# Eight column orders for the moving operand of the matmuls of fourteen weight matrices

## The chip, the cores and the metric

The kernel runs on one core of one Trainium2 chip. The metric is the device time of one execution in microseconds (us). The core has a matrix engine (TensorE, PE in the profile; its weight loads are listed as PEld), a vector engine (DVE), a scalar engine (ACT), GpSimd (POOL) and SyncE (SP), which issues most of the transfers. A matmul first loads a stationary operand into the array and then streams the columns of its moving operand past it; the sums land in a PSUM bank.

## The reference

Two transformer blocks of width 2048 run one after the other on 256 tokens, in fp32. Cut to the products with the fourteen matrices whose layout changes (names of the kernel behind the arrow):

```python
h = rmsnorm(x, g_mix)                        # first block
gate_sb, gate_ca = h @ w_in[...]             # -> w_gsb, w_gca
merged = (sigmoid(gate_sb) * (y_sb @ w_sb_out)      # -> w_sbo
          + sigmoid(gate_ca) * (y_ca @ w_ca_out))   # -> w_cao
x = x + merged @ w_mix_out                   # -> w_mix
x = x + (silu(g_ff) * u_ff) @ w_ffn_out      # -> w_fout
x = x + sigmoid(h @ w_ple_gate) * (p @ w_ple_in)    # -> w_pg
gates = hn @ w_in_2[...]                     # second block -> w_ga, w_gb, w_gc
z = gelu(y) @ w_glu                          # -> w_gluv, w_glug
h = h + merged @ w_out                       # -> w_out
h = h + conv_gated_mlp(...) @ ffn_w_down     # -> w_down
```

All fourteen products have 2048 output columns. Their depths are 2048, except 1024 for `w_sbo`, `w_cao`, `w_gluv` and `w_glug`, 5632 for `w_fout` and 5504 for `w_down`.

## The kernel before

The whole computation is one stream of jobs (`stream`, line 448). A job is one output tile of a product: it reads half tiles of weights, 128 partitions by 1024 fp32, and accumulates into `acc`, two PSUM banks of 512 columns, which exists twice so that the next job can start while the last one is read out.

Each half tile goes through three steps. `load` (L459) is a transfer of 512 KB that SP issues, into one of four `raw` buffers. `high` (L466) rounds it on ACT into `wh`, of type fp32r, a number that one matmul pass can multiply. `low` (L476) subtracts on DVE what was rounded away and rounds that into `wl`. The activations are kept as such a pair too: `hilo` (L318 and L319, or a scaled form at L310 and L313) makes it. A product is then the sum of three passes: high times high, high times low, and low times high. `high` runs four half tiles ahead of the matmuls (five `wh` buffers) and `low` three ahead (four `wl` buffers).

There are two main kinds of job. In a WS job (L526, L530) the weights are the stationary operand and the activations move. In an AS job the activations are stationary and the weights move: `mm_as` (L539) takes, for each of the two 128-row blocks `k` of a half tile and each of the two halves `m` of the 256 tokens, a plain slice of 512 neighbouring columns of `wh` or `wl` and issues three matmuls (L560 to L562). For the very first half tile (L550 to L553) the passes that need `wl` come last. The last job of all calls `mm_as` once per `m` (L509), so that half of the output can be finished early. All matmuls with the fourteen matrices are AS jobs, with four column tiles `n` of 512 columns each. `as_job` (L565) builds them; seven smaller matrices use it too and are not touched by the change.

`_as` (L53) lays an AS matrix out on the host: column tile by column tile, and in it half tile by half tile, 128 partitions by two rows of 512 columns. That is done before the measured time.

The order of the instructions is written out by hand. Beside the job stream, generators (the normalisations, attention heads, gated linear attention, a state-space scan, evacuations of `acc`) advance by one step after each half tile (`tick`); each engine runs its instructions in the order in which they were issued.

Of the kernel before, what the change touches and what calls it, by code (L numbers as in the profile page):

```python
# [35 lines left out]
def _ws(a, b):  # L36

    K, F = a.shape

    def blk(w):  # L40
        return w.reshape(K // 512, 4, 128, F // 128, 128).transpose(3, 0, 2, 1, 4)

    return np.concatenate([blk(a), blk(b)], axis=-1).reshape(-1, 128, 1024)


def _pairs(w):

    K, F = w.shape
    v = w.reshape(K, F // 256, 2, 128)
    return _ws(v[:, :, 0].reshape(K, F // 2), v[:, :, 1].reshape(K, F // 2))  # L50


def _as(w):  # L53
# [19 lines left out]
def layout(x, p, w_in, w_sb_out, w_ca_out, w_mix_out, rel_bias, g_mix, g_ffn, g_ple, g_final, w_ffn_in,  # L73
# [5 lines left out]
    a = {}  # L79
# [5 lines left out]
    i, j = np.arange(128)[:, None], np.arange(128)[None, :]  # L85
# [24 lines left out]
    w = w_in[0]  # L110
# [8 lines left out]

    w = w_in_2[0]  # L120
    a["w_u"] = _pairs(w[:, 0:1024])
    a["w_qkg"] = _ws(w[:, 1024:1536], w[:, 1536:2048])
    a["w_vg"], a["w_r"] = _as(w[:, 2048:3072]), _pairs(w[:, 3072:4096])

    alr = np.zeros((16, 128, 32), np.float32)
# [28 lines left out]
    a["s5b"] = b.reshape(128, 4, 2048).transpose(1, 0, 2)  # L154
    a["s5c"] = c.reshape(128, 2048)
    a["s5bt"] = bt.reshape(128, 2048)
    return {k: np.ascontiguousarray(v) for k, v in a.items()}


# [26 lines left out]
class Build:  # L186
# [261 lines left out]
    def stream(self, jobs):  # L448
        nc = self.nc
        halves = [(j, i, ks) for j in jobs for i, ks in j.halves]  # L450
        N = len(halves)
        raws, spl = {}, {}
        width = lambda j, ks: {"AS": 512 * len(ks), "WS": 1024, "W4": 512}[j.kind]

        def load(i):
            j, idx, ks = halves[i]
            n = width(j, ks)
            r = self.rawp.tile([128, 1024], F32, tag="raw", name=self.name("raw"))
            nc.sync.dma_start(out=r[:, :n], in_=self.d[j.w][idx][:, :n])  # L459
            raws[i] = r  # L460

        def high(i):
            j, idx, ks = halves[i]
            n = width(j, ks)
            wh = self.whp.tile([128, 1024], F32R, tag="wh", name=self.name("wh"))
            nc.scalar.copy(wh[:, :n] if j.kind != "W4" else wh[:, :n].bitcast(F32), raws[i][:, :n])  # L466
            spl[i] = wh

        def low(i):
            j, idx, ks = halves[i]  # L470
            n = width(j, ks)
            r, wh = raws.pop(i), spl[i]
            wl = None
            if j.kind != "W4":
                wl = self.wlp.tile([128, 1024], F32R, tag="wl", name=self.name("wl"))
                nc.vector.tensor_sub(wl[:, :n], r[:, :n], wh[:, :n].bitcast(F32))  # L476
            spl[i] = (wh, wl)
            if i + RAWB < N:
                load(i + RAWB)

        ahead = self.at_start(load)
        for i in range(CA):
            next(ahead)
            high(i)
            if i < SA:
                low(i)
        self.add(ahead)
        last, prev, acc = None, None, None
        for i, (j, idx, ks) in enumerate(halves):
            if i + CA < N:  # L490
                high(i + CA)
            if i + SA < N:
                low(i + SA)
            if j is not last:
                if j.before is not None:
                    j.before()
                while prev is not None and not prev.free:
                    self.tick(must=True)
                prev, last = last, j
                acc = self.accp.tile([128, 2, 512], F32, tag="acc", name=self.name("acc"))  # L500
            for k in ks:
                while k not in j.acts.ready:
                    self.tick(must=True)
            first, end = j.halves[0][1][0], j.halves[-1][1][-1]
            if j.by_m is not None:

                for m in range(2):
                    for q, (_, _, kq) in enumerate(halves[i:]):
                        self.mm_as(j.acts, kq, *spl[i + q], acc, (m,), first, end)  # L509
                    j.by_m(m, acc)  # L510
                break
            wh, wl = spl.pop(i)
            if j.kind == "AS":
                self.mm_as(j.acts, ks, wh, wl, acc, (0, 1), first, end, low_last=i == 0)
            elif j.kind == "W4":

                for k in range(16):
                    p = slice(32 * (k % 4), 32 * (k % 4) + 32)
                    nc.tensor.matmul(acc[p, 0, :], lhsT=wh[:, 32 * k:32 * k + 32].bitcast(F32),
                                     rhs=j.acts.at(k).bitcast(F32), start=k < 4, stop=k >= 12)  # L520
            else:
                for kk, k in enumerate(ks):
                    x = j.acts.at(k)
                    for f in range(2):
                        s = slice((kk * 2 + f) * 128, (kk * 2 + f) * 128 + 128)
                        hi = lambda: nc.tensor.matmul(  # L526
                            acc[:, f, :], lhsT=wh[:, s], rhs=x, start=k == first, stop=k == end)
                        if k == first:
                            hi()
                        nc.tensor.matmul(acc[:, f, 256:512], lhsT=wl[:, s], rhs=x[:, 0:256], start=False, stop=False)  # L530
                        if k != first:
                            hi()
            if i + 1 == N or halves[i + 1][0] is not j:
                self.add(j.evac(acc, lambda j=j: setattr(j, "free", True)), front=True)
            self.tick()
        while self.gens:
            self.tick(must=True)

    def mm_as(self, acts, ks, wh, wl, acc, ms, first, end, low_last=False):  # L539

        nc = self.nc
        if low_last:
            for low in (False, True):
                for kk, k in enumerate(ks):
                    s = slice(kk * 512, kk * 512 + 512)
                    for m in ms:
                        x = acts.at(k)
                        xh, xl = x[:, m * 128:m * 128 + 128], x[:, 256 + m * 128:384 + m * 128]
                        if low:
                            nc.tensor.matmul(acc[:, m, :], lhsT=xh, rhs=wl[:, s], start=False, stop=False)  # L550
                        else:
                            nc.tensor.matmul(acc[:, m, :], lhsT=xl, rhs=wh[:, s], start=k == first, stop=False)
                            nc.tensor.matmul(acc[:, m, :], lhsT=xh, rhs=wh[:, s], start=False, stop=False)  # L553
            return
        for kk, k in enumerate(ks):
            x = acts.at(k)
            s = slice(kk * 512, kk * 512 + 512)
            for m in ms:
                xh, xl = x[:, m * 128:m * 128 + 128], x[:, 256 + m * 128:384 + m * 128]
                nc.tensor.matmul(acc[:, m, :], lhsT=xl, rhs=wh[:, s], start=k == first, stop=False)  # L560
                nc.tensor.matmul(acc[:, m, :], lhsT=xh, rhs=wl[:, s], start=False, stop=False)  # L561
                nc.tensor.matmul(acc[:, m, :], lhsT=xh, rhs=wh[:, s], start=False, stop=k == end)  # L562


    def as_job(self, w, n, acts, evac, k0=0, nk=None, before=None, kt=None):  # L565

        kt = kt or acts.n
        nk = nk or acts.n
        per = (kt + 1) // 2
        halves = [(n * per + (k0 + k) // 2, list(range(k, min(k + 2, nk)))) for k in range(0, nk, 2)]  # L570
        return Job("AS", w, halves, acts, lambda acc, free: evac(n, acc, free), before)

    def ws_job(self, w, j, acts, evac, before=None):

# [1193 lines left out]
```

## Time and profile before

| | us |
|---|---|
| median of 2 runs | 3183.36 (3183.13 to 3183.58) |
| profiled execution, its own time | 3182.36 |
| its span | 3180.2 |
| PE busy | 3161.4 |
| DVE busy | 1994.4 |
| ACT busy | 1553.3 |

The span runs from the first to the last instruction. A line of the groups view names the source line, the engine, the operation, its output and inputs by tile name, the shape and the count; behind the bar stand the busy time in us, the mean duration of one in ns, and how long the engine had been idle just before, with what ended that wait. A line `min/median/max` gives durations in ns, and then the first and the last start in us from the span's beginning. A windows line gives, for one stretch, the busy time and the number of instructions of each engine, the granted clock of TensorE, and the share and the rate of the DMA engines. The matmuls overlap, so that their busy times add up to more than the time in which they run; a line of the page counts overlapping time once.

### The profile page before, as it was taken

To read this page: it belongs to the slowest core of one execution; us is meant where nothing else is said; L and a number is where in the kernel's file an instruction comes from. 1 tells how busy PE (TensorE), PEld (TensorE's weight loads), DVE (VectorE), ACT (ScalarE), POOL (GpSimd) and SP (SyncE) were. 2 spreads that over 40 slices of the span, in tenths; PEclk is the share of its full clock that TensorE was granted. 3 is DMA by queue.
4 is the path that set the end of the run, shared out by engine and by line. 5 is a ranking of instruction groups with operands and counts; after the bars stand their busy time and mean duration, and the time that the engine had idled before them with its cause. 6 is when DMAs were issued, how large, how long until landed. Compare 5 with 4: busy or idle time off the path is not lost.

```text
span 3180.2 us, 43735 instructions
## 1 busy us (share of the span) xinstructions
PE 3161.4 (99%) x16909; PEld 2668.2 (84%) x16909; DVE 1994.4 (63%) x2593; ACT 1553.3 (49%) x2035; POOL 72.5 (2%) x158
## 2 busy tenths in 40 slices
PE   8999999999999999999999999999999999999998
PEld 7888888888888888888888888878888888888887
DVE  5656445557577676566655657945555766757666
ACT  6544444455444454456544454434445644545545
POOL 0000000000001000000000001000000000000000
PEclk9999999999999999999999999999999999999999
DMA  7555555565667767555654565655555555555554
GB/s 263 168 176 166 185 188 183 180 187 186 216 223 246 243 225 238 186 175 190 210 178 159 170 214 192 211 183 198 197 183 182 186 192 185 186 195 185 189 185 165
DMA packets 172639, 617.90 MB, mean 194 GB/s; under 512 B 23552, under 2 KB 23968, under 8 KB 169232
## 3 DMA queue, kind: packets, MB, share of 16 engines
q1 hardware_dynamic: 164992, 577.49, 55.8%
q0 software_dynamic: 7440, 37.64, 3.5%
q8 instruction: 132, 2.16, 0.3%
q14 instruction: 75, 0.61, 0.1%
HBM read 599.74 MB, written 14.25 MB: 193 GB/s over the span
## 4 chain that ended last, share of the span: by engine, by line
PE 99%; ACT 0%; DMA 0%; DVE 0%; DVEq 0%; issue 0%; SPq 0%; ACTq 0%
PE acc L526 29%; PE acc L560 17%; PE acc L562 17%; PE acc L561 17%; PE acc L530 15%; PE p L346 1%; PE p L1673 0%; PE p L1132 0%; PE p L1713 0%; PE p L906 0%; PE p L908 0%; PE p L907 0%; PE p L1716 0%; PE p L1109 0%; PE p L1128 0%; PE p L1707 0%
## 5 line engine op out<-in xcount | busy, mean ns | idle before, releaser
L476 DVE TENSOR_TENSOR wl<-raw,wh 128x1024 fp32r<-128x1024 f32 x1088 | 1320.6, 1220 | 667.1 <-PE acc L561 446.0
L466 ACT CAST wh<-raw 128x1024 fp32r<-128x1024 f32 x1088 | 1138.9, 1049 | 1110.3 <-PE acc L562 672.1
L526 PE MATMUL acc<-s,wh 128*128 128x512 f32 x3936 | 1383.8, 396 | 0.0
L530 PE MATMUL acc<-s,wl 128*128 128x256 f32 x3936 | 1090.6, 282 | 0.0
L560 PE MATMUL acc<-wh,s 128*128 128x512 f32 x2372 | 939.0, 396 | 0.8 <-DVE big L1351 0.8
L562 PE MATMUL acc<-wh,s 128*128 128x512 f32 x2372 | 930.8, 392 | 0.0
L561 PE MATMUL acc<-wl,s 128*128 128x512 f32 x2372 | 930.3, 392 | 0.0
L526 PEld LDWEIGHTS acc<-s,wh 128*128 128x128 f32 x3936 | 734.1, 188 | 164.0
L530 PEld LDWEIGHTS acc<-s,wl 128*128 128x128 f32 x3936 | 741.7, 188 | 11.0 <-issue 1.0
L562 PEld LDWEIGHTS acc<-wh,s 128*128 128x128 f32 x2372 | 445.6, 188 | 99.9
L560 PEld LDWEIGHTS acc<-wh,s 128*128 128x128 f32 x2372 | 445.9, 188 | 99.2 <-issue 1.7
L561 PEld LDWEIGHTS acc<-wl,s 128*128 128x128 f32 x2372 | 446.0, 188 | 97.5 <-issue 0.5
L442 DVE TENSOR_TENSOR s<-acc,s 128x512 f32<-128x512 f32 (+1 forms) x120 | 82.7, 689 | 271.1 <-ACT s L441 271.0
L441 ACT COPY s<-acc 128x512 f32<-128x512 f32 (+1 forms) x120 | 70.0, 584 | 195.0 <-PE acc L526 192.8
L310 ACT ACTIVATE s<-s 128x256 f32<-128x256 f32 (+4 forms) x175 | 76.6, 443 | 105.2 <-DVE s L313 38.1
L313 DVE SCALAR_TENSOR_TENSOR s<-s,conv 128x256 f32<-128x256 f32 x172 | 79.4, 482 | 3.1
L444 DVE TENSOR_TENSOR s<-s,rb 128x512 f32<-128x512 f32 (+1 forms) x104 | 71.7, 690 | 3.5
L318 ACT CAST s<-s 128x256 fp32r<-128x256 f32 (+1 forms) x104 | 45.5, 442 | 30.4 <-DVE s L946 15.3
L1630 DVE TENSOR_TENSOR s<-s,s 128x1024 f32<-128x1024 f32 x48 | 58.5, 1219 | 0.0
L310 ACT ACTIVATE s<-s,conv 128x256 f32<-128x256 f32 x86 | 47.1, 595 | 22.5 <-DVE s L444 22.5
L319 DVE TENSOR_TENSOR s<-s,s 128x256 fp32r<-128x256 f32 (+1 forms) x104 | 47.4, 458 | 14.2 <-ACT s L318 13.0
L310 ACT ACTIVATE junk<-big 128x512 f32<-128x512 f32 x48 | 30.3, 632 | 50.0 <-DVE big L925 35.5
(265 smaller groups left out, 1034.5 us busy)
## 6 DMA issues: line engine op xcount, KB each, us to landing
raw<-in_w_fin SPq DMA_DIRECT2D x176, 512.0 KB, 4.3
raw<-in_w_up SPq DMA_DIRECT2D x172, 512.0 KB, 3.9
raw<-in_w_fout SPq DMA_DIRECT2D x88, 512.0 KB, 4.2
raw<-in_w_down SPq DMA_DIRECT2D x84, 512.0 KB, 4.0
raw<-in_w_qksb SPq DMA_DIRECT2D x32, 512.0 KB, 3.6
raw<-in_w_qkca SPq DMA_DIRECT2D x32, 512.0 KB, 3.4
raw<-in_w_gsb SPq DMA_DIRECT2D x32, 512.0 KB, 4.2
raw<-in_w_gca SPq DMA_DIRECT2D x32, 512.0 KB, 4.2
```

The lines of the kernel that those rows point to most:

```text
L310: self.nc.scalar.activation(out, in_, func, scale=scale, **kw)
L313: self.nc.vector.scalar_tensor_tensor(out=out, in0=in0, scalar=scalar, in1=in1, op0=op0, op1=op1)
L441: nc.scalar.copy(out, acc[:, 0:n, 256:512])
L442: nc.vector.tensor_add(out, acc[:, 0:n, 0:256], out)
L444: nc.vector.tensor_mul(out, out, rb.tile[:, None, :].to_broadcast([128, n, 256]) if n > 1 else rb.tile[:, None, :])
L466: nc.scalar.copy(wh[:, :n] if j.kind != "W4" else wh[:, :n].bitcast(F32), raws[i][:, :n])
L476: nc.vector.tensor_sub(wl[:, :n], r[:, :n], wh[:, :n].bitcast(F32))
L526: hi = lambda: nc.tensor.matmul(acc[:, f, :], lhsT=wh[:, s], rhs=x, start=k == first, stop=k == end)
L530: nc.tensor.matmul(acc[:, f, 256:512], lhsT=wl[:, s], rhs=x[:, 0:256], start=False, stop=False)
L560: nc.tensor.matmul(acc[:, m, :], lhsT=xl, rhs=wh[:, s], start=k == first, stop=False)
L561: nc.tensor.matmul(acc[:, m, :], lhsT=xh, rhs=wl[:, s], start=False, stop=False)
L562: nc.tensor.matmul(acc[:, m, :], lhsT=xh, rhs=wh[:, s], start=False, stop=k == end)
```

## The change

The moving operand of an AS matmul is no longer always a plain row of 512 columns. A table `WALKS` holds eight orders, each a nest of (step, count) from the outermost to the innermost; the first is the plain row. `WALK_OF` names fourteen matrices and gives an order for each of their four column tiles. On the host, `_walked` moves the columns of each row of 512 to the places at which the order will visit them, so that the t-th column visited is column t of the product. In the kernel, `moving` gives the matmul a view of the same row in `wh` or `wl` with the steps of the order. The accumulator is written as before, one column after another. For instance, order 3, `((2, 128), (256, 2), (1, 2))`, reads two neighbouring columns at 0, two at 256, two at 2, two at 258, and so on.

`mm_as` takes the job in place of its activations, since it needs the matrix's name and the column tile, and its two loop nests become one; the matmuls that it issues and their order stay.

```diff
+WALKS = (
+    ((1, 512),),
+    ((8, 32), (256, 2), (1, 8)),
+    ((4, 64), (256, 2), (1, 4)),
+    ((2, 128), (256, 2), (1, 2)),
+    ((2, 2), (4, 128), (1, 2)),
+    ((16, 2), (32, 16), (1, 16)),
+    ((16, 4), (64, 8), (1, 16)),
+    ((4, 2), (8, 64), (1, 4)),
+)
+WALK_OF = {"w_gsb": (1, 2, 3, 4), "w_gca": (5, 6, 7, 0), "w_sbo": (1, 2, 3, 4), "w_cao": (5, 6, 7, 0),
+           "w_mix": (1, 2, 3, 4), "w_fout": (5, 6, 7, 0), "w_pg": (1, 2, 3, 4), "w_ga": (5, 6, 7, 0),
+           "w_gb": (1, 2, 3, 4), "w_gc": (5, 6, 7, 0), "w_gluv": (1, 2, 3, 4), "w_glug": (5, 6, 7, 0),
+           "w_out": (0, 1, 2, 3), "w_down": (4, 5, 6, 7)}
+
+def walk(w, n):
+    return WALKS[WALK_OF[w][n]] if w in WALK_OF else WALKS[0]
+
+def _walked(halves, name):
+    per = halves.shape[0] // 4
+    out = np.empty_like(halves)
+    for n in range(4):
+        at = np.zeros(1, np.int64)
+        for step, count in walk(name, n):
+            at = (at[:, None] + step * np.arange(count)).reshape(-1)
+        src, dst = (t[n * per:n * per + per].reshape(per, 128, 2, 512) for t in (halves, out))
+        dst[..., at] = src
+    return out
...
+    for name in WALK_OF:
+        a[name] = _walked(a[name], name)
...
-    def mm_as(self, acts, ks, wh, wl, acc, ms, first, end, low_last=False):
...
+    def moving(self, j, w, kk):
+        v = w[:, kk * 512:kk * 512 + 512]
+        wk = walk(j.w, j.n)
+        if len(wk) == 1:
+            return v
+        names = "abcd"[:len(wk)]
+        order = sorted(range(len(wk)), key=lambda i: -wk[i][0])
+        grouped = " ".join(names[i] for i in order)
+        return v.rearrange(f"p ({grouped}) -> p {' '.join(names)}", **{names[i]: wk[i][1] for i in range(len(wk))})
+
+    def mm_as(self, j, ks, wh, wl, acc, ms, first, end, low_last=False):
+        nc, acts = self.nc, j.acts
+        steps = [(kk, k, m) for kk, k in enumerate(ks) for m in ms]
+        passes = ((False,), (True,)) if low_last else ((False, True),)
+        for part in passes:
+            for kk, k, m in steps:
+                x = acts.at(k)
                 xh, xl = x[:, m * 128:m * 128 + 128], x[:, 256 + m * 128:384 + m * 128]
+                bh, bl = self.moving(j, wh, kk), self.moving(j, wl, kk)
+                if part == (True,):
+                    nc.tensor.matmul(acc[:, m, :], lhsT=xh, rhs=bl, start=False, stop=False)
+                    continue
+                nc.tensor.matmul(acc[:, m, :], lhsT=xl, rhs=bh, start=k == first, stop=False)
+                if True in part:
+                    nc.tensor.matmul(acc[:, m, :], lhsT=xh, rhs=bl, start=False, stop=False)
+                nc.tensor.matmul(acc[:, m, :], lhsT=xh, rhs=bh, start=False, stop=k == end and True in part)
...
+        job = Job("AS", w, halves, acts, lambda acc, free: evac(n, acc, free), before)
+        job.n = n
+        return job
```

More of the change, by code (lines that the diff above doesn't have):

```diff
@@ L508, in stream @@
                     for q, (_, _, kq) in enumerate(halves[i:]):
-                        self.mm_as(j.acts, kq, *spl[i + q], acc, (m,), first, end)
+                        self.mm_as(j, kq, *spl[i + q], acc, (m,), first, end)
                     j.by_m(m, acc)
@@ L513, in stream @@
             if j.kind == "AS":
-                self.mm_as(j.acts, ks, wh, wl, acc, (0, 1), first, end, low_last=i == 0)
+                self.mm_as(j, ks, wh, wl, acc, (0, 1), first, end, low_last=i == 0)
             elif j.kind == "W4":
@@ L537, in stream @@
             self.tick(must=True)
-    def mm_as(self, acts, ks, wh, wl, acc, ms, first, end, low_last=False):
[L541 to L558, printed above, removed]
-                xh, xl = x[:, m * 128:m * 128 + 128], x[:, 256 + m * 128:384 + m * 128]
-                nc.tensor.matmul(acc[:, m, :], lhsT=xl, rhs=wh[:, s], start=k == first, stop=False)
-                nc.tensor.matmul(acc[:, m, :], lhsT=xh, rhs=wl[:, s], start=False, stop=False)
-                nc.tensor.matmul(acc[:, m, :], lhsT=xh, rhs=wh[:, s], start=False, stop=k == end)
@@ L570, in as_job @@
         halves = [(n * per + (k0 + k) // 2, list(range(k, min(k + 2, nk)))) for k in range(0, nk, 2)]
-        return Job("AS", w, halves, acts, lambda acc, free: evac(n, acc, free), before)
+        job = Job("AS", w, halves, acts, lambda acc, free: evac(n, acc, free), before)
+        job.n = n
+        return job
     def ws_job(self, w, j, acts, evac, before=None):
```

## The prediction

> **What bounds the kernel now.** I read the page's first lines and its summary of the chain that ended last.
>
> ```profile
> span 3180.2 us, 43735 instructions
> PE 3161.4 (99%) x16909; PEld 2668.2 (84%) x16909; DVE 1994.4 (63%) x2593; ACT 1553.3 (49%) x2035; POOL 72.5 (2%) x158
> PEclk9999999999999999999999999999999999999999
> PE 99%; ACT 0%; DMA 0%; DVE 0%; DVEq 0%; issue 0%; SPq 0%; ACTq 0%
> ```
>
> The matmuls are 99% of the chain, in every slice, at the full granted clock. So whatever a matmul gains or loses moves the end by the same amount, and nothing covers it. The groups by line show which matmuls the change reaches, and who feeds them.
>
> ```profile
> L560 PE MATMUL acc<-wh,s 128*128 128x512 f32 x2372 | 939.0, 396 | 0.8 <-DVE big L1351 0.8
> L562 PE MATMUL acc<-wh,s 128*128 128x512 f32 x2372 | 930.8, 392 | 0.0
> L561 PE MATMUL acc<-wl,s 128*128 128x512 f32 x2372 | 930.3, 392 | 0.0
> L476 DVE TENSOR_TENSOR wl<-raw,wh 128x1024 fp32r<-128x1024 f32 x1088 | 1320.6, 1220 | 667.1 <-PE acc L561 446.0
> L466 ACT CAST wh<-raw 128x1024 fp32r<-128x1024 f32 x1088 | 1138.9, 1049 | 1110.3 <-PE acc L562 672.1
> ```
>
> The three lines L560 to L562 are all matmuls of the AS jobs but 12 of the first half tile, and each streams 512 columns of a weight tile. PE never sat idle before them (0.8 us in all), while the engines that prepare `wh` and `wl` sat idle 1110 and 667 us, mostly until PE released a buffer. PE does not wait for its operands.
>
> The mean of 392 to 396 ns is how long one matmul takes from start to end, and matmuls overlap. What counts is the distance between starts. I took a stretch that holds only AS matmuls: the windows view says what else ran in it, the view of line L560 where its first and its last matmul start.
>
> ```profile
> 2271.50:2315.90 44.40, 44.40 (x199) 36.48 (x197) 23.62 (x22) 20.64 (x22) 0.11 (x1) 1.00 0.56 190
> ```
> ```profile
> L560 PE MATMUL acc<-wh,s x64: 388/390/475, 2271.9 to 2315.3; 128*128 128x512 f32 x64
> ```
>
> From 2271.9 to 2315.3 us lie 63 steps of L560, each of three matmuls: 43.4 us / 189 = 229.6 ns per matmul, at a granted clock of 1.00. That is 0.448 ns per column: 0.90 ns for two columns, 1.79 ns for four. This pace is the number that the change puts at stake.
>
> **What does not change.** The weights are permuted on the host, outside the measured time; each load keeps its 512 KB, in the same place of SP's queue. `high` and `low` still cast and subtract whole contiguous rows. The merged `mm_as` issues the same matmuls in the same order, the first half tile's included. No instruction, wait, buffer or output address is added, and output column t still goes to column t of the accumulator. All of that I cost at nothing, with no cover needed, because nothing of it is moved. What changes is the address from which PE takes each moving column.
>
> **How many matmuls change.** Per 128 rows of a matrix and per column tile n there are 6 matmuls (two m, three products). Counting 128-row blocks: the matrices with orders (1,2,3,4) have 16+8+16+16+16+8 = 80, those with (5,6,7,0) have 16+8+44+16+16+8 = 108, `w_out` with (0,1,2,3) 16 and `w_down` with (4,5,6,7) 43. So order 0 gets 124 blocks or 744 matmuls, orders 1, 2 and 3 get 96 or 576 each, order 4 gets 123 or 738, and orders 5, 6 and 7 get 151 or 906 each: 5928 matmuls, of which 5184 no longer read contiguously. Per matmul, the runs of adjacent columns are 64 of eight (order 1), 128 of four (2 and 7), 256 of two (3 and 4) and 32 of sixteen (5 and 6).
>
> **What a run costs.** No matmul of this kernel reads its moving columns from scattered places, so the trace has no price for it. The nearest rows are elementwise instructions of ACT and DVE that read fp32 elements which are not neighbours. In the S5 stage L318 on ACT and L319 on DVE read 256 elements per partition at steps of 64 elements, and L1172 on DVE reads two inputs at steps of 4. Beside them stand the contiguous ones: all of L318 (its median is contiguous), and L946. The lines come from the views of single lines, the DVE timeline around 2112 us, and the groups by shape.
>
> ```profile
> L318 ACT CAST s<-s x104: 388/404/681, 695.8 to 3138.1; 128x256 fp32r<-128x256 f32 x95, 128x512 fp32r<-128x512 f32 x9
> L318 ACT CAST s<-s x4: 657/660/681, 2110.9 to 2113.6; 128x256 fp32r<-128x256 f32 x4
> ```
> ```profile
> 2113.83 1.15 DVE L319 TENSOR_TENSOR s<-s,s 128x256 fp32r<-128x256 f32 x2
> ```
> ```profile
> L466 ACT CAST wh<-raw 128x1024 fp32r<-128x1024 f32 x1084 | 1136.5, 1051 | 1104.1 <-PE acc L562 667.4 <-PE acc L526 230.2 <-issue 87.3
> ```
> ```profile
> L476 DVE TENSOR_TENSOR wl<-raw,wh 128x1024 fp32r<-128x1024 f32 x1084 | 1318.0, 1222 | 667.1 <-PE acc L561 446.0 <-PE acc L530 90.1 <-issue 68.3
> L946 DVE TENSOR_TENSOR s<-s 128x256 f32<-128x256 f32 x44 | 18.4, 419 | 4.7 <-ACT s L310 4.7
> L1172 DVE TENSOR_TENSOR s<-u,rb 128x256 f32<-128x256 f32 x8 | 4.6, 616 | 0.2
> ```
>
> A contiguous element costs ACT (1051 - 404)/768 = 0.84 ns and DVE (1222 - 419)/768 = 1.05 ns. A lone element costs more by (660 - 404)/256 = 1.00 ns on ACT, (616 - 419)/256 = 0.77 ns in L1172 and (575 - 419)/256 = 0.61 ns in L319. Added up, fetching from a new place takes 1.84, 1.82 and 1.66 ns. Two engines of different speed arrive at nearly one time; it looks like a time of the memory, not a number of engine cycles. And contiguous fp32 runs at 1.79 ns per four columns on PE: no row of this trace shows an engine read that needs new places faster than that.
>
> So I cost a run on PE as the longer of two times: its fetch, about 1.77 ns (the mean of the three), and its streaming, 0.448 ns per column. A run of four streams for 1.79 ns, one of eight or sixteen for longer; orders 1, 2, 5, 6 and 7 then cost nothing. A run of two streams for 0.90 ns and has to wait for its fetch: 256 x 1.77 = 453 ns per matmul in place of 229.6, or 223.5 ns more. Orders 3 and 4 together have 576 + 738 = 1314 matmuls, so 294 us. The bounds from the lowest and the highest row are 256 x 1.66 = 425 ns, which gives 257 us, and 256 x 1.84 = 471 ns, which gives 317 us.
>
> Across mechanisms the bounds are wider. Below: as many columns still pass through the array, and the quickest contiguous matmul (388 ns) is 2 ns shorter than the median (390), so a gain beyond 5184 x 2 ns = 10 us has no room. Above: every run, however long, pays the extra 0.61 to 1.00 ns, priced in the second rival.
>
> **The sum.** The profiled execution took 3182.4 us, 2.2 us of it outside the span. 3182.4 + 294 = 3476 us, by its bounds 3439 to 3500; the median before is 1.0 us above the profiled execution, which I leave inside the rounding. What is late next: nothing new. ACT and DVE get more time per half tile and wait longer for PE; PE remains 99% of the chain.
>
> **Rivals.** *The pair is enough* (not slower). PE's port may fetch from a new place within the time of two columns, because it already takes four columns in the time that ACT and DVE need for a lone element, and because those rows price only lone elements: on ACT a pair would stream for 2 x 0.84 = 1.68 ns, which covers its fetch almost completely, and none of the eight orders reads fewer than two neighbours at a time. What decides is the fetch time of a run of two: at 0.90 ns or less nothing changes and the time is 3182 us; 64 us, the 2% mark, is reached at 229.6 + 49 = 278 ns per matmul or 1.09 ns per run. Against it: 0.90 is half of every fetch time in the rows. [...]
>
> *Every jump costs.* If contiguous lines are fetched ahead and a jump breaks that, each run adds its extra wait on top of streaming. The runs are 576 x (64 + 128 + 256) + 738 x 256 + 906 x (32 + 32 + 128) = 620,928; at 0.61 to 1.00 ns they add 379 to 621 us: 3561 to 3803 us, about 3680. For it: the lone elements pay on top of their streaming. Against it: steps of 4 elements (L1172) and of 64 cost DVE about the same, so distance alone does not show.
>
> *In between*: a fetch of a pair in 1.0 to 1.6 ns gives 3220 to 3430 us. *No effect at all*: the permuted view could be issued as a plain row; the outputs would then be wrong, so I give that next to nothing, at 3182 us.
>
> **How the numbers follow.** The forecast (only runs of two pay) gets 0.43; the pair being enough, with the no-effect case, 0.37; every jump 0.13; in between 0.05; some unforeseen gain 0.02. The predicted time is the forecast's 3476 us. The range must take in both 3182 and the forecast's 3500, since each holds over a third: 3176 to 3510 us, which leaves out every-jump and the gain, 0.15. The forecast's own range is 3439 to 3500. A measurement of this kernel can tell about 2% (64 us) from no change. Slower by over 2%: 0.43 + 0.13 + 0.05 = 0.61; within: 0.37; faster: 0.02.
>
> **What will show it.** The column tiles n of one matrix stand next to each other in time with one order each, so the distance between matmul starts can be read order by order: `w_out` gives orders 0 to 3, each group of `w_down` orders 4 to 7. The forecast says about 230 ns for 0, 1, 2, 5, 6 and 7, and 425 to 471 ns for 3 and 4. The forecast is wrong if 3 and 4 keep 230 ns, or if 2 and 7 slow down too; the first would make PE's fetch at least twice as quick as that of ACT and DVE, the second would make jumps the cost. The waits of ACT and DVE on PE should grow by what PE loses, and the granted clock should stay at 1.00.

## The result and the profile after

The changed kernel takes 3443.82 us (3443.06 to 3444.57), the kernel before 3183.36 us: a ratio of 1.082, 95% interval 1.0794 to 1.0846, or 260.5 us more. Its profiled execution took 3443.06 us, with a span of 3441.2 us.

The page of the changed kernel: first lines, chain that ended last, and the groups that answer to those shown above. L600, L602 and L603 are the old L560, L561 and L562; L600 and L603 now take in eight of the first half tile's matmuls as well.

```profile
span 3441.2 us, 43735 instructions
PE 3423.2 (99%) x16909; PEld 2694.5 (78%) x16909; DVE 1999.2 (58%) x2593; ACT 1555.8 (45%) x2035; POOL 72.5 (2%) x158
PEclk9999999999999999999999999999999999999999
PE 99%; ACT 0%; DMA 0%; DVE 0%; DVEq 0%; issue 0%; SPq 0%; ACTq 0%
L513 DVE TENSOR_TENSOR wl<-raw,wh 128x1024 fp32r<-128x1024 f32 x1088 | 1322.0, 1221 | 877.3 <-PE acc L602 647.1
L503 ACT CAST wh<-raw 128x1024 fp32r<-128x1024 f32 x1088 | 1140.8, 1050 | 1348.0 <-PE acc L603 900.6
L563 PE MATMUL acc<-s,wh 128*128 128x512 f32 x3936 | 1384.3, 397 | 0.0
L600 PE MATMUL acc<-wh,s 128*128 128x512 f32 x2376 | 1036.7, 436 | 8.6 <-ACT wh L503 7.8
```

The span grew by 261.0 us, PE's busy time by 261.8 us, and ACT and DVE kept theirs (1553.3 to 1555.8 us, 1994.4 to 1999.2 us): as many instructions, at the same granted clock (0.999 over both spans), and PE still 99% of the chain. The WS matmuls (L563) kept their 396 to 397 ns. ACT and DVE only wait longer for PE (1348 and 877 us instead of 1110 and 667). All of the loss is in the AS matmuls, and none of it is a wait for operands.

Which order costs what can be read where one matrix goes through its column tiles. The view of line L600 in stretches of `w_out` (orders 0, 1, 2 and 3, from top to bottom) and of the second group of `w_down` (orders 4, 5, 6 and 7):

```profile
L600 PE MATMUL acc<-wh,s x24: 388/390/475, 2545.9 to 2561.6; 128*128 128x512 f32 x24
L600 PE MATMUL acc<-wh,s x28: 403/407/489, 2566.0 to 2585.8; 128*128 128x512 f32 x28
L600 PE MATMUL acc<-wh,s x28: 411/418/511, 2590.3 to 2610.7; 128*128 128x512 f32 x28
L600 PE MATMUL acc<-wh,s x28: 501/506/573, 2616.2 to 2642.8; 128*128 128x512 f32 x28
L600 PE MATMUL acc<-wh,s x24: 612/632/635, 2999.8 to 3031.0; 128*128 128x512 f32 x24
L600 PE MATMUL acc<-wh,s x24: 398/404/420, 3032.3 to 3048.9; 128*128 128x512 f32 x24
L600 PE MATMUL acc<-wh,s x24: 394/403/412, 3049.6 to 3066.2; 128*128 128x512 f32 x24
L600 PE MATMUL acc<-wh,s x24: 392/397/398, 3066.9 to 3082.9; 128*128 128x512 f32 x24
```

The first and the last start lie 23 (or 27) steps of three matmuls apart: order 0 has 15.7 us / 69 = 228 ns between starts, order 3 26.6 us / 81 = 328 ns, order 4 31.2 us / 69 = 452 ns. Taken over all pairs of neighbouring AS matmuls of an order in the trace, the means are:

| order | runs per matmul | ns between starts | above order 0 | matmuls | us |
|---|---|---|---|---|---|
| 0 | 1 of 512 | 230.6 | | 744 | |
| 1 | 64 of 8 | 246.1 | 15.5 | 576 | 8.9 |
| 2 | 128 of 4 | 251.6 | 21.0 | 576 | 12.1 |
| 3 | 256 of 2, to and fro by 256 columns | 330.0 | 99.4 | 576 | 57.3 |
| 4 | 256 of 2, forward by 4 columns | 452.6 | 222.0 | 738 | 163.8 |
| 5 | 32 of 16 | 240.2 | 9.6 | 906 | 8.7 |
| 6 | 32 of 16 | 239.4 | 8.8 | 906 | 8.0 |
| 7 | 128 of 4 | 234.0 | 3.4 | 906 | 3.1 |

The last column adds up to 262 us, for 260.5 us measured. Two things are not as forecast: order 3 pays less than half of what order 4 pays, though both read runs of two, and the long runs cost a little too.

### The profile page after: what moved, and what is told of

The parts are those of the page before. It is cut to its first block, busy times and chain, and to the rows that moved or that the text cites. A ratio compares the mean times of both kernels' runs of the same rounds, so it can differ in the third digit from the quotient of the medians.

```text
span 3441.2 us, 43735 instructions
## 1 busy us (share of the span) xinstructions
PE 3423.2 (99%) x16909; PEld 2694.5 (78%) x16909; DVE 1999.2 (58%) x2593; ACT 1555.8 (45%) x2035; POOL 72.5 (2%) x158
## 4 chain that ended last, share of the span: by engine, by line
PE 99%; ACT 0%; DMA 0%; DVE 0%; DVEq 0%; issue 0%; SPq 0%; ACTq 0%
PE acc L563 27%; PE acc L600 18%; PE acc L603 18%; PE acc L602 18%; PE acc L567 14%; PE p L383 1%; PE p L1716 0%; PE p L1175 0%; PE p L1756 0%; PE p L949 0%; PE p L950 0%; PE p L951 0%; PE p L1759 0%; PE p L1152 0%; PE p L1171 0%; PE p L1750 0%
## 5 line engine op out<-in xcount | busy, mean ns | idle before, releaser
L563 PE MATMUL acc<-s,wh 128*128 128x512 f32 x3936 | 1384.3, 397 | 0.0
L600 PE MATMUL acc<-wh,s 128*128 128x512 f32 x2376 | 1036.7, 436 | 8.6 <-ACT wh L503 7.8
L603 PE MATMUL acc<-wh,s 128*128 128x512 f32 x2376 | 1028.6, 433 | 0.0
L602 PE MATMUL acc<-wl,s 128*128 128x512 f32 x2372 | 1025.9, 433 | 0.0
L563 PEld LDWEIGHTS acc<-s,wh 128*128 128x128 f32 x3936 | 735.1, 188 | 164.0 <-issue 0.5
L600 PEld LDWEIGHTS acc<-wh,s 128*128 128x128 f32 x2376 | 455.5, 192 | 184.2 <-issue 60.8
L603 PEld LDWEIGHTS acc<-wh,s 128*128 128x128 f32 x2376 | 455.3, 192 | 178.9 <-issue 60.7
L602 PEld LDWEIGHTS acc<-wl,s 128*128 128x128 f32 x2372 | 454.1, 191 | 174.3 <-issue 58.4
L1016 DVE TENSOR_TENSOR big<-big,acc 128x1024 f32<-128x1024 f32 x24 | 29.3, 1221 | 50.8 <-PE acc L603 50.8
```

Source lines behind the costliest of these rows:

```text
L563: hi = lambda: nc.tensor.matmul(acc[:, f, :], lhsT=wh[:, s], rhs=x, start=k == first, stop=k == end)
L600: nc.tensor.matmul(acc[:, m, :], lhsT=xl, rhs=bh, start=k == first, stop=False)
L602: nc.tensor.matmul(acc[:, m, :], lhsT=xh, rhs=bl, start=False, stop=False)
L603: nc.tensor.matmul(acc[:, m, :], lhsT=xh, rhs=bh, start=False, stop=k == end and True in part)
```

## The experiments

In the first four and in the tests of streams only the table `WALKS` is another; the layout follows it, and so the outputs stay. One run then gives seven orders beside the plain row, which kept 230.5 to 230.8 ns in each of them. Times between starts below are means over all neighbouring matmuls of an order. Theory A is the one on record: a run costs one fetch of about 1.77 ns.

**Runs of two, at seven steps**

```diff
-    ((8, 32), (256, 2), (1, 8)),
...
+    ((2, 2), (4, 128), (1, 2)),
+    ((2, 4), (8, 64), (1, 2)),
+    ((2, 8), (16, 32), (1, 2)),
+    ((2, 16), (32, 16), (1, 2)),
+    ((2, 32), (64, 8), (1, 2)),
+    ((2, 64), (128, 4), (1, 2)),
+    ((2, 128), (256, 2), (1, 2)),
```

> Only the table of orders is another: order 0 plain, orders 1 to 7 read runs of two columns whose starts step by S = 4, 8, 16, 32, 64, 128, 256 columns (order 1 is the order 4 of the changed kernel, 453 ns between matmul starts there; order 7 its order 3, 328 ns). In all of them every run of two goes to another group of four columns than the run before; they differ in how many other groups are visited before the second half of a group is read: 127, 63, 31, 15, 7, 3, 1. Theory A, each run of two costs one fetch of about 1.77 ns whatever the order, as predicted: about 453 ns for all seven (already at odds with the 328 ns of S = 256). Theory B, a fetch costs about 1.7 ns, and the last two groups of four columns are held, so that a return after one other group is free: 453 ns for S = 4 to 128 and 328 for S = 256 alone. Theory C, fetches overlap when they go to places far apart: a time that falls step by step, or at one bit of the step, between S = 4 and S = 256, with S = 128 (512 bytes apart) near 328 ns.

Measured, for S = 4 to 256: 455, 462, 433, 458, 492, 445 and 330 ns, in a kernel of 4251 us. Line L600 in `w_down`, for S = 64, 128 and 256:

```profile
L600 PE MATMUL acc<-wh,s x24: 683/689/696, 3737.5 to 3771.2; 128*128 128x512 f32 x24
L600 PE MATMUL acc<-wh,s x24: 634/636/646, 3772.7 to 3803.3; 128*128 128x512 f32 x24
L600 PE MATMUL acc<-wh,s x24: 503/506/520, 3804.7 to 3827.3; 128*128 128x512 f32 x24
```

There is no gradual fall with the distance (C): 512 bytes are as dear as 16, and only the order that comes back after one other place is cheap, as B says. What B does not say is the spread of 433 to 492 ns.

**Runs of four, at six steps**

> Only the table of orders is another: order 0 plain, orders 1 to 6 read runs of four columns whose starts step by S = 8, 16, 32, 64, 128, 256 columns (S = 8 is the changed kernel's order 7, 233 ns there, S = 256 its order 2, 250 ns), order 7 is the plain row written as runs of sixteen. Theories A and B, one fetch of about 1.7 ns per group of four: 229 to 250 ns for all six, with the small excess unexplained. Theory C, fetches depend on the distance between consecutive places: differences between the six that follow the step as those of the runs of two do. A third account of the small excess, that a nest of three counts costs something by itself: all six alike at 233 to 250 ns. Order 7: 229 ns in every account.

Measured for S = 8 to 256: 235, 227, 247, 278, 268 and 251 ns; the plain row written as a nest 231 ns; the kernel 3279.7 us. Even the dearest run of four costs 47 ns over the plain row, where runs of two cost 202 to 261 ns at the same steps but the last. So a run of four is close to the plain row at every step, and a run of two is not. The excess neither grows nor falls steadily with the step, and S = 16, a nest of three counts with a jump after every fourth column, has none at all: it is no price of the nest, and none of a jump.

**Longer runs**

> Only the table of orders is another: order 0 plain, orders 1 to 3 read runs of eight columns whose starts step by 16, 64 and 256 columns, orders 4 to 6 runs of sixteen with steps of 32, 128 and 256, order 7 is the plain row written as a nest of (256, 2), (16, 16), (1, 16). Theories A and B: 229 to 250 ns for all. If the excess of 4 to 22 ns that the changed kernel shows in its orders 1, 2, 5, 6 and 7 belongs to the jumps, runs of sixteen (32 jumps) should cost less than runs of eight (64); if it belongs to the nest itself, both should cost the same, and order 7 too if its nest is not merged into a plain row (about 240 ns, else 229).

Measured: runs of eight at steps of 16, 64 and 256 columns 235, 248 and 244 ns; runs of sixteen at 32, 128 and 256 columns 240, 233 and 241 ns; the plain row as a nest 231 ns; the kernel 3220.3 us. Fewer jumps do not cost clearly less. The plain row written as a nest decides nothing: the trace lists its operand as one count of 512, so it reached PE as a plain row, here and in the run before. That a nest of three counts is free rests on the runs of four at S = 16 (227 ns) and the runs of sixteen at 128 (233 ns). What sets the excess of 2 to 18 ns stayed open.

**Single columns**

```diff
+    ((1, 2), (2, 256)),
+    ((1, 4), (4, 128)),
+    ((1, 8), (8, 64)),
+    ((1, 16), (16, 32)),
+    ((1, 64), (64, 8)),
+    ((1, 128), (128, 4)),
+    ((1, 256), (256, 2)),
```

> Only the table of orders is another: order 0 plain, orders 1 to 7 read single columns at steps of 2, 4, 8, 16, 64, 128 and 256 columns. Theory A, one fetch of 1.77 ns per run: about 906 ns for all seven. Theory B, fetches of 1.7 ns, two groups of four columns held: step 2 reads two columns of each group in turn, 256 fetches, 453 ns; steps 4 to 128 need a fetch for every column, 870 to 906 ns; step 256 reads every group once, 128 fetches and otherwise held columns, under 453 ns or, if a lone column cannot be taken faster than a pair, about 430 to 460. Theory C: a fall with the distance from step 4 to step 256.

Measured, in that order: 455, 462, 432, 433, 491, 283 and 217.5 ns; the kernel 3983.1 us, faster than with runs of two. Line L600 in `w_out` at a step of 2, and in `w_down` at steps of 128 and 256:

```profile
L600 PE MATMUL acc<-wh,s x28: 632/632/691, 2990.8 to 3027.4; 128*128 128x512 f32 x28
L600 PE MATMUL acc<-wh,s x24: 447/451/476, 3557.0 to 3576.5; 128*128 128x512 f32 x24
L600 PE MATMUL acc<-wh,s x24: 379/379/383, 3577.3 to 3592.2; 128*128 128x512 f32 x24
```

All three theories fall here. A lone column costs no more than a pair: 432 to 491 ns at steps of 2 to 64, not 906. And the order that jumps 256 columns at every single step is the quickest seen so far, 14.9 us / 69 = 216 ns, below the plain row. In that order the 1st, 3rd, 5th column are 0, 1, 2, and the 2nd, 4th, 6th are 256, 257, 258. That led to theory D, an estimate from these times and not a thing that a trace lists: PE reads two columns at a time, through two streams, each with its own groups of four columns (16 bytes). A stream that finds only one column in each group needs two steps for it; with two or more it keeps up. By it each stream finds two columns per group in the plain row (229 ns), four in the order above (216 ns), and only one in a run of two (453 ns in order 4).

**Where a run starts**

```diff
-            wh = self.whp.tile([128, 1024], F32R, tag="wh", name=self.name("wh"))
+            wh = self.whp.tile([128, 1026], F32R, tag="wh", name=self.name("wh"))[:, 2:]
```

> The changed kernel's eight orders, but each wh buffer starts 8 bytes (two columns) later; the wl buffers stay, so the matmuls of wl are the control in the same run. Theory D, built on the runs so far: PE takes the columns two at a time, the first and the second of each two through a stream of their own; a stream that reads two or more columns from the same aligned group of four before it leaves it keeps the pace, and a group that is visited for one column costs two steps instead of one. Shifted by two columns, a run of four lies in two groups: orders 2 and 7 go from 250 and 233 ns to about 430 to 460 for wh. A run of eight touches three groups for four columns of a stream, order 1 about 320 ns; a run of sixteen five for eight, orders 5 and 6 about 270 ns. Order 0 stays near 229 and order 4 at 453; wl is unchanged in all. Theory F, only the length of a run counts and not where it starts: wh and wl alike, as in the changed kernel (244, 250, 328, 453, 240, 240, 233 ns).

Measured between the start of a `wh` matmul (L600) and the next, and after a `wl` matmul (L602): order 0 238 and 234, order 1 366 and 254, order 2 340 and 255, order 3 333 and 328, order 4 454 and 454, order 5 286 and 246, order 6 292 and 242, order 7 456 and 253 ns. The kernel took 3722 us. Lines L600 and L602 in the same stretch of order 7, and of order 5:

```profile
L600 PE MATMUL acc<-wh,s x24: 617/634/647, 3311.7 to 3338.1; 128*128 128x512 f32 x24
L602 PE MATMUL acc<-wl,s x24: 411/415/418, 3312.1 to 3338.5; 128*128 128x512 f32 x24
L600 PE MATMUL acc<-wh,s x24: 446/450/469, 3272.5 to 3291.2; 128*128 128x512 f32 x24
L602 PE MATMUL acc<-wl,s x24: 402/406/416, 3272.8 to 3291.5; 128*128 128x512 f32 x24
```

The same run of four costs twice as much when it starts two columns later (order 7, 456 ns for 234). So, by these times, the group is an aligned one of 16 bytes, and the length of a run is not what counts; F falls. By D's numbers orders 0, 4, 5, 6 and 7 came out near (270 expected for 5 and 6, 286 and 292 measured), order 1 higher (366 for 320), and order 2 much lower, 340 for 430 to 460. In the shifted order 2 each group is read once, left for two others, and read again, so this points to a stream that still holds a group after two others. The control did not stay put either: after a `wl` matmul orders 7, 1 and 2 took 253, 254 and 255 ns, for 232, 243 and 250 in the changed kernel. A slow matmul seems to cost its neighbour something, and no run separates the two; 21 ns at most are small beside the 222 ns that order 7 lost.

**Two streams, at seven distances**

```diff
+    ((4, 128), (1, 2), (2, 2)),
+    ((8, 64), (1, 4), (4, 2)),
+    ((16, 32), (1, 8), (8, 2)),
+    ((32, 16), (1, 16), (16, 2)),
+    ((64, 8), (1, 32), (32, 2)),
+    ((128, 4), (1, 64), (64, 2)),
+    ((256, 2), (1, 128), (128, 2)),
```

> Only the table of orders is another. Orders 1 to 7 read single columns in turn from two places r = 2, 4, 8, 16, 32, 64 and 128 columns apart, r columns from each, and then the next 2r: for r = 4 it is 0, 4, 1, 5, 2, 6, 3, 7, then 8. The single columns with a step of 256 took 216 ns, less than the plain row. Theory D, two streams, one for the first and one for the second of each two columns: for r = 4 and more each stream reads all four columns of a group before it leaves it, 216 ns or a few ns above for all six; r = 2 gives each stream two columns of every group, as the plain row does: 229 ns. Theory G, what helps is the distance between the two places: 216 ns near r = 128 only, and 229 to 460 ns for the short ones.

Measured for r = 2: 233 ns, which the same column tiles also take as plain rows in the kernel before; for r = 4 to 128: 217.2, 216.4, 216.4, 215.9, 216.5 and 217.4 ns; the kernel 3119.5 us, faster than the kernel before. Line L600, r = 2 and 4 in `w_out` and r = 128 in `w_down`:

```profile
L600 PE MATMUL acc<-wh,s x28: 389/389/479, 2335.0 to 2353.5; 128*128 128x512 f32 x28
L600 PE MATMUL acc<-wh,s x28: 379/379/463, 2357.6 to 2375.2; 128*128 128x512 f32 x28
L600 PE MATMUL acc<-wh,s x24: 379/379/379, 2778.4 to 2793.3; 128*128 128x512 f32 x24
```

D held in all seven. G fails from r = 4 on: four columns apart, in neighbouring groups, is as good as 128. The difference is whether a stream reads two or four columns of a group before it goes on. With four, the durations hardly vary (379/379/379 for r = 128).

**How many groups a stream holds**

```diff
+    ((8, 64), (1, 2), (2, 4)),
+    ((16, 32), (1, 4), (4, 4)),
+    ((64, 8), (1, 16), (16, 4)),
+    ((256, 2), (1, 64), (64, 4)),
+    ((32, 16), (1, 4), (4, 8)),
+    ((128, 4), (1, 16), (16, 8)),
+    ((64, 8), (1, 4), (4, 16)),
```

> Only the table of orders is another. Single columns in turn from p places, r columns apart, r columns from each: orders 1 to 4 have p = 4 and r = 2, 4, 16, 64, so that each of the two streams of theory D goes to and fro between two groups of four columns (and reads two columns of each in order 1, four in 2 to 4); orders 5 and 6 have p = 8 and r = 4 and 16 (four groups per stream in turn), order 7 p = 16 and r = 4 (eight groups). If a stream holds two groups: about 328 ns in order 1 and 283 ns in 2 to 4, as steps of 256 pairs and 128 single columns gave, and 430 to 490 ns in 5 to 7. If it holds one only, orders 1 to 4 go to 430 to 490 ns, and the 283 and 328 ns belonged to the distance of 1024 bytes. If it holds more than two, 5 and 6 fall below 430 ns.

Measured: order 1 342 ns, orders 2 to 4 270, 270 and 283 ns, orders 5 to 7 480, 440 and 462 ns. Line L600 in `w_down` for order 4 (two groups per stream) and order 5 (four):

```profile
L600 PE MATMUL acc<-wh,s x24: 438/451/451, 3420.5 to 3440.0; 128*128 128x512 f32 x24
L600 PE MATMUL acc<-wh,s x24: 649/668/668, 3440.8 to 3473.9; 128*128 128x512 f32 x24
```

The simplest account is that a stream that goes to and fro between two groups keeps both, whichever distance was tried, and among four keeps none that it needs again. That is order 3: its streams read groups a, b, a, b, so half of the visits need no fetch, and it costs 330 ns instead of 453. An estimate from these runs: where a stream changes group at every column and holds two, it fetches 64 times per matmul (270 to 283 ns), 128 times (330 to 342 ns) or 256 times (432 to 492 ns), and each step fits about 0.9 ns per fetch on top of 216 ns. The plain row also fetches 128 times per stream and takes only 229 ns, so a fetch is nearly hidden when the two columns of a group come one right after the other, and not when another group comes between them (330 to 342 ns). The streams and what they hold are inferred from times alone. The shifted order 2 would need three groups held, which no other order tried.

**Runs of two undone**

```diff
-    ((2, 128), (256, 2), (1, 2)),
-    ((2, 2), (4, 128), (1, 2)),
+    ((1, 512),),
+    ((1, 512),),
```

> Undo one part: orders 3 and 4, the runs of two, are replaced by the plain row; orders 1, 2, 5, 6 and 7 stay. By the distances between starts in the changed kernel the five that stay cost 576 x (15.5 + 21.0) + 906 x (9.6 + 8.8 + 3.4) ns = 41 us over the plain row, and orders 3 and 4 the remaining 222 us: 3224 us. The prediction as it stood (only runs of two pay) says 3183 us. If single matmuls and the time of the kernel were only loosely tied, it would be neither.

Measured: 3223.16 us, ratio to the kernel before 1.0125 (1.0108 to 1.0142), 39.8 us against 3183.36 and 40.3 against the 3182.86 us measured beside it. So orders 3 and 4 make 221 us of the 260.5, the other five 40 us; times between starts add up to the time of the kernel.

**A better order for all AS matrices**

```diff
+    ((1, 256), (256, 2)),
...
+WALK_OF = {w: (1, 1, 1, 1) for w in (
+    "w_vsb", "w_vca", "w_gsb", "w_gca", "w_sbo", "w_cao", "w_mix",
+    "w_fout", "w_pin", "w_pg", "w_vg", "w_vd", "w_brb", "w_brc",
+    "w_ga", "w_gb", "w_gc", "w_gluv", "w_glug", "w_out", "w_down")}
```

> All 21 matrices of the AS jobs are read as single columns with a step of 256 (0, 256, 1, 257, and so on). If the 216 ns that one column tile showed hold everywhere and PE stays the bound, 7128 matmuls gain about 13.5 ns each: 96 us, 3087 us, 0.970 of the kernel before. If the gain needs slower neighbours (operands that arrive with more lead), PE begins to wait for wh or wl and less of it is left: between 3087 and 3183 us.

Measured: 3083.56 us, ratio 0.9688 (0.9674 to 0.9703). The page's groups, and line L594 (the old L560) in `w_down`:

```profile
L497 ACT CAST wh<-raw 128x1024 fp32r<-128x1024 f32 x1088 | 1136.8, 1048 | 1026.6 <-PE acc L597 555.3
L594 PE MATMUL acc<-wh,s 128*128 128x512 f32 x2376 | 910.1, 383 | 8.8 <-ACT wh L497 8.0
```
```profile
L594 PE MATMUL acc<-wh,s x24: 379/379/379, 2711.8 to 2726.7; 128*128 128x512 f32 x24
```

The gain is 99 us for 96 expected, and PE did not begin to wait: of the 8.8 us before L594, 8.0 lie at the very start and 0.8 near the end, where the kernel before waited 8.6 us (L552) and 0.8 us (L560).

**And for the WS matmuls**

```diff
+                    xm = x.rearrange("p (h b a) -> p h a b", h=2, b=2)
+                    xhm = x[:, 0:256].rearrange("p (b a) -> p a b", b=2)
...
-                            acc[:, f, :], lhsT=wh[:, s], rhs=x, start=k == first, stop=k == end)
+                            acc[:, f, :], lhsT=wh[:, s], rhs=xm, start=k == first, stop=k == end)
...
-                        nc.tensor.matmul(acc[:, f, 256:512], lhsT=wl[:, s], rhs=x[:, 0:256], start=False, stop=False)
+                        nc.tensor.matmul(acc[:, f, 256:512], lhsT=wl[:, s], rhs=xhm, start=False, stop=False)
...
+            o = out.rearrange("p n (b a) -> p n b a", b=2)
+            hi, lo = (acc[:, 0:n, c:c + 256].rearrange("p n (a b) -> p n b a", b=2) for c in (0, 256))
+            nc.scalar.copy(o, lo)
+            nc.vector.tensor_add(o, hi, o)
```

> As the kernel that reads all AS matrices as single columns with a step of 256, and the moving operand of the WS matmuls too is read from two places in turn, 128 columns apart in each half of 256 (0, 128, 1, 129, and so on); the sums land in that order of the tokens, and the two instructions on ACT and DVE that add the two halves put them back in order. By theory D a WS matmul of 512 columns goes from 233 to 217 ns and one of 256 from 118 to 109 ns, 3936 of each: 16 + 9 ns x 3936 = 98 us less, 2985 us. The reads of PSUM at every other column cost ACT and DVE up to 0.6 to 1.0 ns per element, some 0.3 to 0.5 us for each of 120 pairs, off PE's path. The rival: those reads, or operands that now come too late, make PE wait, and the time stays near 3084 us.

Measured: 2991.71 us, ratio 0.9398 (0.9383 to 0.9414), 192 us less than the kernel before and 92 us less than with the AS matmuls alone, for 98 expected. The page's groups for the WS matmuls and for the two instructions that read PSUM at every other column:

```profile
L565 PE MATMUL acc<-s,wh 128*128 128x512 f32 x3936 | 1294.3, 383 | 0.0
L569 PE MATMUL acc<-s,wl 128*128 128x256 f32 x3936 | 1058.3, 274 | 0.0
L479 DVE TENSOR_TENSOR s<-acc,s 128x512 f32<-128x512 f32 x119 | 82.3, 691 | 222.9 <-ACT s L478 222.8
L478 ACT COPY s<-acc 128x512 f32<-128x512 f32 x119 | 69.7, 586 | 158.9 <-PE acc L565 158.5
```

The WS matmuls fell from 396 and 282 ns to 383 and 274 ns; between starts, from medians of 233 and 118 ns to 218 and 109 ns. The reads of PSUM cost nothing extra: 586 ns on ACT and 691 on DVE, where the same shape read contiguously took 586 and 692 ns in the kernel before.

## Why the prediction was right, and where it was not

The time (3443.8 us in a range of 3176 to 3510), the sign and the place came out: AS matmuls alone, no new wait, PE still the chain, ACT and DVE waiting longer, the clock unchanged at 0.999. The size came out near, 260 us for 294, and inside the bounds of 257 to 317, but partly by luck: two of its terms were wrong in opposite directions, and the lower bound rests on a misread row.

- *Nothing else costs.* Held: as many instructions, unchanged WS matmuls, and the sum over orders within 2 us of the kernel's difference.
- *A run of two waits for its fetch, 453 ns per matmul.* Right for order 4 (452.6 ns, 164 us for 165), wrong for order 3 (330 ns, 57 us for 129). The step that failed is "256 x 1.77 = 453 ns" for both orders alike: it took the run as the unit. The runs fit two streams with aligned groups of 16 bytes, of which a stream keeps at least two (270 to 283 ns to and fro between two whole groups, 440 to 480 ns among four); order 3 comes back to a group after one other.
- *Orders 1, 2, 5, 6 and 7 cost nothing.* They cost 41 us by the sum over orders, 40 us with orders 3 and 4 undone. This missing term and the oversized one of order 3 (71 us too much) went against each other, which is why the sum is closer (294 for 260) than its parts. The excess appears where a stream reads two columns of a group and then jumps, and is gone with four (216 to 217 ns); why it changes with the step between 0 and 47 ns is not settled.
- *The fetch time from ACT and DVE, 1.66 to 1.84 ns.* That it met order 4 to half a nanosecond is luck. The 575 ns of L319 are half of a timeline row in which two instructions overlap; each alone took 612 to 633 ns, as the line below shows. With 620 ns the fetch time of L319 is 1.83 ns, the three rows give 1.82 to 1.84 ns, and the forecast becomes 469 ns per matmul and 314 us (311 to 317), which misses the 260 us. Measured runs of two that return to no held group took 433 to 492 ns, which no single fetch time gives. And the reading that a lone element pays on its own, as on ACT and DVE, was wrong for PE: single columns at steps of 2 to 64 took 432 to 491 ns, pairs at steps of 4 to 128 433 to 492.
- *The pair is enough* was wrong: with the columns counted as they come it leaves order 4 at 229 ns, and order 4 took 452.6. Counted for each stream of theory D a pair fits the runs better: the plain row gives each stream two columns of a group, a run of two gives each one. Even so two are not quite full pace here: 229 ns, and 216 with four.
- *Every jump costs* was wrong: single columns that jump 256 columns at every step take 216 ns.
- *In between.* Its band, worked out again from a fetch of 1.0 to 1.6 ns, is 3217 to 3419 us, not 3220 to 3430. The stretch taken for the pace also holds a few transposes (L346), all ahead of its first AS matmul. Nothing hangs on either.
- *A gain beyond 10 us has no room.* Wrong as a bound, though not for these eight orders. The step was to take the quickest contiguous matmul (388 ns) as the floor; 379 ns is possible, and over all AS matmuls that is 99 us.

The view of line L319 in the kernel before, from 2110 to 2116 us:

```profile
L319 DVE TENSOR_TENSOR s<-s,s x4: 612/620/633, 2111.6 to 2114.4; 128x256 fp32r<-128x256 f32 x4
```

## What to carry to other kernels

A bound taken from the best case of the present form (here the quickest contiguous matmul) says nothing about other forms; a table of orders that are cheap to vary, each in its own column tile, priced seven forms per run and found one that beat the plain row. Where fp32r columns stream past the array back to back, lay them out so that the 1st, 3rd, 5th and the 2nd, 4th, 6th column each come from contiguous memory, at least four columns from a place aligned to 16 bytes: 216 ns instead of 229 per 512 columns here, and 6% of the whole kernel with the AS and the WS matmuls. No run of that layout had another start, so what one would cost was not shown. When the parts of a forecast can err in both directions, check them one by one even if the sum fits.

## What the runs showed of the hardware

The plain row is not the quickest way to read a moving operand of fp32r: 229 ns between starts against 216 ns, with durations that hardly vary (379/379/379 in one stretch). Single columns from two places in turn are as quick at 16 bytes' distance as at 1024 (217.2 and 217.5 ns). In order 7 a run of four that starts 8 bytes off its group costs 456 ns instead of 234. Reads of every other fp32 from PSUM cost ACT and DVE nothing (586 and 691 ns for 512, as contiguous ones), while reads of SBUF at steps of 16 and of 256 bytes cost 0.77 to 1.00 ns more per element than contiguous ones. The steps differ too, so the runs do not show whether the memory or the step makes the difference.
